# Forgetting attention's value matmuls with two heads in turn, and retention's scores in head order, in a two-layer hybrid decoder

## The chip, the core and the metric

One core of a Trainium2 chip runs the whole program: two decoder layers, one launch. The metric is the time of one execution in device microseconds (us). The core's engines work side by side, each through its own queue in order: PE (TensorE, with its weight loads, PEld), DVE (VectorE), ACT (ScalarE), POOL (GpSimd) and SP, which issues most DMAs. They wait for one another through semaphores.

## What is computed

The input is 512 tokens of width 1024; 16 learned meta tokens are put ahead of them. Each of two layers projects the normalized state, runs three mixers side by side (retention, a multi-scale pooling, and forgetting attention), projects their output, adds and normalizes, and then runs a SwiGLU. The reference for the parts that matter here, shortened:

```python
def retention_chunkwise(q, k, v):          # 4 heads, dk 48, dv 96, chunks of 128
    ...
    scores = jnp.einsum('bnihd,bnjhd->bnhij', qc, kc) * dmask
    inner = jnp.einsum('bnhij,bnjhe->bnihe', scores, vc)
    ...

def forgetting_attention(q, k, v, logf):   # 6 heads of 64, blocks of 128 queries
    ...
    def block(ib):
        s = jnp.einsum('bihd,bjhd->bhij', qb, kf)
        s = s + cb[..., :, None] - c[..., None, :]
        s = jnp.where(mask, s, NEG_INF)
        p = jax.nn.softmax(s, axis=-1)
        return jnp.einsum('bhij,bjhd->bihd', p, vf)
    ...
```

## The kernel before

The 528 positions are five chunks: chunk 0 holds the 16 meta tokens, chunks 1 to 4 hold 128 tokens each (`CH`). Two column halves, "A" (chunks 0 to 2) and "B" (3 and 4), go through the projections one after the other. Projection weights come in by DMA, are split by ACT (L188) and DVE or POOL (L140) into a high and a low part, and three matmuls (L241 to L243) do each product; these make up most of PE's work.

The order of PE's work is set by a planner. The program adds pieces with a cost in us, a priority, and for each dependency a lag (`LAG`); `Plan.run` keeps a clock of its own, takes at each step the ready piece of best priority, and adds its cost. It also counts what a piece holds until another has run (`holds`): buffers named "tmp" (7), "y" (23), "one" (PSUM banks) and so on. PE executes its instructions in this order (`manual_schedule`); the instructions of the other engines are issued by the same pieces. Projection pieces have priority 9 and attention pieces 5 and less, so projections fill the time in which attention has nothing ready.

Forgetting attention of chunk c (1 to 4) goes over six heads. For each head, `fox_score` makes the logits (two matmuls for each stretch of keys, L694 and L695), DVE adds the mask and finds the maximum (L739), ACT takes the exponential (L740), DVE normalizes (L741, L742) and POOL scales the meta tokens' share, pm (L743). `fox_turn` transposes the result in blocks of 128 keys (L751); DVE copies it back for even heads and ACT for odd ones (L753). `fox_value` multiplies it with the values of these c blocks (L761), one matmul for each block, adding up in PSUM. Each has 64 output rows: an even head writes partitions 0 to 63 and an odd one 64 to 127 of the same bank. Each fp32 matmul leaves two records in the trace. `fox_meta` adds the meta tokens' share (L774) and writes the result for the output projection (mixAf, mixBf). The copy of the transposed block of a head is held in a "tmp" buffer until its `fox_value` has run.

Retention of a chunk is `ret_score` (L816: four heads; heads 0 and 1 sit in rows 0 to 63 and 64 to 127 of one tile, heads 2 and 3 of another, and even heads write one PSUM bank, odd heads a second), `ret_out` and `ret_turn`; `ret_mix` later multiplies with the gate (L870) and splits the result for the output projection (ACT L872; the low part xl by DVE, or by POOL for the second of the three tiles). At the end of a mixing stage, `whole` adds the two parts of the layer's input on POOL (L420, 16 instructions), since the space is then reused for the mixers' output; `pool_mix` runs pooling's own matmuls (L901); and the output projection (L241 to L243 from mixAf, xh and xl) begins.

Of the kernel before, what the change touches and what calls it, by code (L numbers as in the profile page):

```python
# [17 lines left out]
P = 128  # L18
# [41 lines left out]
class Plan:  # L60
# [6 lines left out]
    def add(self, fn, cost=0.0, deps=(), prio=None):  # L67
        self.n += 1
        p = Piece(fn, cost, [d for d in (d if isinstance(d, tuple) else (d, 0.0) for d in deps) if d[0] is not None],
                  (5 if prio is None else prio, self.n))  # L70
        self.open.append(p)
        return p
# [34 lines left out]
def hymba_kernel(ctx: ExitStack, tc: tile.TileContext, d: dict, out: bass.AP):  # L107
    nc = tc.nc
# [21 lines left out]
    def one():  # L130
        return ps_one.tile([P, 512], F32, tag="one", name="one")
# [390 lines left out]
    def mixing(l, x, ready, ap_):  # L522

        def lag(k):
            return LAG.get(f"{k}_{l}", LAG[k])
# [10 lines left out]
        def tmp(name, shape=(P, NM + T), view=None):  # L536
            t = ap_.tile([P, NM + T], F32, tag="tmp", name=name, bufs=7)
            return t

        mix, F = {}, {}  # L540
# [13 lines left out]
        def open_mix():  # L554
            for half in "AB":
# [8 lines left out]
        vt = {"vf": ap_.tile([P, 4, 384], F32, tag="vtf", name="vtf"),  # L564
              "vr": ap_.tile([P, 5, 384], F32, tag="vtr", name="vtr")}
# [186 lines left out]
            pt = F[c, "pt", h] = ap_.tile([P, 512], F32, tag="tmp", name="pt", bufs=7)  # L752
            (nc.scalar.copy if h % 2 else nc.vector.tensor_copy)(pt[:, :nk], tp[:, :nk])  # L753

        def fox_value(c, h):
            nk = CH[c][1] - NM
            if h == 0:
                F[c, "o"] = one()
            o, pt = F[c, "o"], F.pop((c, "pt", h))
            for b in range(nk // P):  # L760
                nc.tensor.matmul(o[64 * (h % 2):64 * (h % 2) + 64, (h // 2) * P:(h // 2 + 1) * P],  # L761
                                 lhsT=vt["vf"][:, b, h * 64:(h + 1) * 64], rhs=pt[:, b * P:(b + 1) * P],
                                 start=(h < 2 and b == 0), stop=False, skip_group_check=True)

        def fox_meta(c, step):
            if step == 0:
# [42 lines left out]
        def ret_score(c):  # L809
            cs, ce = CH[c]  # L810
            n = ce - cs
            s = [one(), one()]
            for h in (0, 2, 1, 3):
                r0 = 64 * (h % 2)
                ab = "AB"[h // 2]
                nc.tensor.matmul(s[h % 2][:n, P * (h // 2):P * (h // 2) + n], lhsT=qk["k" + ab][r0:r0 + 64, cs:ce],  # L816
                                 rhs=qk["q" + ab][r0:r0 + 64, cs:ce], start=True, stop=True)
            if c:
                qx = R["qx", c] = tmp("qx")[:, :256].rearrange("p (j i) -> p j i", j=2)
                for j, ab in enumerate("AB"):  # L820
                    nc.vector.tensor_tensor(qx[:, j, :n], qk["q" + ab][:, cs:ce], C["xi"][:, j, :n], op=ALU.mult)
            pt = R["pt", c] = tmp("rpt")[:, :512].rearrange("p (b a i) -> p b a i", b=2, a=2)
            for b in range(2):
                nc.vector.tensor_tensor(pt[:n, b, :, :n], s[b][:n, :256].rearrange("p (a i) -> p a i", a=2)[:, :, :n],
                                        C["dm"][:n, b, :, :n], op=ALU.mult)
# [86 lines left out]
        def n_of(half, key):  # L912
# [3 lines left out]
        add = plan.add  # L916
# [10 lines left out]
        vf = {c: add(lambda c=c: v_turn("vf", c), 0.35, at(hf[c], "vt", *[("vf", i) for i in range(3)]), 3)  # L927
              for c in range(5)}
# [37 lines left out]
        if 0 in qch:  # L966
# [8 lines left out]
            b = add(lambda: fox_first(1), 0.05, [(a, lag("a"))], 5)  # L975
            mixes[0] = add(lambda: fox_first(2), 0.05, [(b, lag("b")), (vf[0], lag("v0")), oa], 5)
        prev_v, ss = None, [None, None]
        for c in range(1, 5):
            nk = ce = CH[c][1]
            for h in range(6):  # L980
                if h % 2 == 0:
                    qp = queries(c, h // 2)
                sc_ = add(lambda c=c, h=h: fox_score(c, h), 0.02 + max(ce, NA) / 1200.0,
                          at("AB"[:1 + (c > 2)], "kb", ("kf", h // 2))
                          + [(qp, lag("q")), ss[-1] if c == 4 else ss[-2]] + fb, 5)
                if h % 2:
                    qp.holds("Q", 1, sc_)
                ss.append((sc_, lag("s") + nk / 530.0))
                tn = add(lambda c=c, h=h: fox_turn(c, h), 0.11 * (nk // P), [(sc_, lag("p") + nk / 450.0)], 5)
                prev_v = add(lambda c=c, h=h: fox_value(c, h), 0.16 * (nk // P),  # L990
                             [(tn, lag("pt")), prev_v] + [(vf[b], lag("vt")) for b in range(1, c + 1)], 5)
                sc_.holds("tmp", 2, tn)
                tn.holds("tmp", 1, prev_v)
                if h == 0:
                    first_v = prev_v
            mt = add(lambda c=c: fox_meta(c, 0), 0.11, [(sc_, lag("p") + nk / 450.0)], 5)
            mixes[c] = prev_v = add(lambda c=c: fox_meta(c, 1), 0.65, [(mt, lag("mt")), prev_v, (vf[0], lag("v0"))]
                                    + [of if c > 2 else oa], 5)
            first_v.holds("one", 1, prev_v)
# [418 lines left out]
    with tc.tile_pool(name="at1", bufs=1) as ap_:  # L1418
        load_consts(1, ap_)
        x, ready, hs, keep = mixing(1, x, ready, ap_)  # L1420
# [122 lines left out]
```

## Time and profile before

| what | us |
|---|---|
| median of 3 runs | 1224.96 |
| lowest and highest run | 1223.85, 1227.76 |
| the profiled execution's own time | 1226.59 |
| its span, first to last instruction | 1224.8 |
| attention's value matmuls, L761, busy on PE | 30.3 |
| attention's transposes, L751, busy on PE | 21.3 |
| retention's scores, L816, busy on PE | 6.7 |

The span is one profiled execution; what lies around it is 1226.59 - 1224.8 = 1.8 us. A row of the timeline has the start in us from the span's start, the duration, the engine, the line and operation, out<-in by the program's names, and the count; where the engine sat idle before, the length and the releaser follow in brackets. Neighbouring matmuls overlap in the records, since a matmul's record lasts longer than the time after which the next can start. Where a row counts several, the duration is from the first start to the last end. A stretch's row has the busy time of each engine within it and, in brackets, its records.

### The profile page before, as it was taken

How to read it: one execution, taken by the hardware profiler on the slowest of the kernel's cores; microseconds unless marked ns; L12 is line 12 of the kernel's file. 1: busy time of each engine (PE TensorE's matmuls, PEld its weight loads, DVE VectorE, ACT ScalarE, POOL GpSimd, SP SyncE). 2: the span in 40 equal slices, each digit the busy share in tenths (PEclk: the TensorE clock that was granted, in tenths of full speed). 3: DMA queues.
4: the chain of work that ended last, by engine and by line, in shares of the span. 5: the costliest groups of instructions: out<-in, count | busy, mean ns of one | idle time of the engine just before them, and what ended most of it. 6: DMA issues, size and time to landing. Idle time of an engine off the chain costs nothing. (4 is left out here: it accounts for less than half of the span.)

```text
span 1224.8 us, 23583 instructions
## 1 busy us (share of the span) xinstructions
PE 1187.4 (97%) x9154; PEld 1135.8 (93%) x9154; DVE 833.3 (68%) x1762; ACT 600.7 (49%) x1178; POOL 322.1 (26%) x383
## 2 busy tenths in 40 slices
PE   7999999989999999999999899999999999999996
PEld 6999989989999999999999899999899999998885
DVE  6575686899885268864675655778897777763337
ACT  5535554466663236653355265445665555552222
POOL 5423446251110011100054243373311111100004
PEclk9999999999999999999999999999999999999999
DMA  6332201547762367732434221124477777532222
GB/s 240 108 107 70 71 18 58 170 135 177 193 162 81 100 186 180 179 82 84 130 114 130 80 74 59 43 91 160 139 193 198 181 181 181 140 115 91 93 96 69
DMA packets 58944, 151.90 MB, mean 124 GB/s; under 512 B 8328, under 2 KB 16808, under 8 KB 58832
## 3 DMA queue, kind: packets, MB, share of 16 engines
q1 hardware_dynamic: 47888, 130.46, 33.3%
q0 software_dynamic: 10944, 19.93, 10.1%
q8 instruction: 72, 1.18, 0.4%
q14 instruction: 40, 0.33, 0.1%
HBM read 144.38 MB, written 2.10 MB: 120 GB/s over the span
## 5 line engine op out<-in xcount | busy, mean ns | idle before, releaser
L241 PE MATMUL acc<-xh,w 128*128 128x256 f32 (+1 forms) x1024 | 299.7, 293 | 5.8 <-DVE ka L140 3.9
L242 PE MATMUL acc<-xl,w 128*128 128x256 f32 (+1 forms) x1024 | 291.3, 284 | 0.4 <-DVE xl L905 0.4
L243 PE MATMUL acc<-xh,w 128*128 128x256 f32 (+1 forms) x1024 | 291.3, 284 | 0.0
L140 DVE TENSOR_TENSOR w<-raw,w 128x1024 fp32r<-128x1024 f32 (+3 forms) x236 | 226.6, 978 | 68.2 <-ACT w L188 64.8
L188 ACT CAST w<-raw 128x1024 fp32r<-128x1024 f32 (+1 forms) x176 | 176.1, 1002 | 153.9 <-PE acc L243 86.5
L241 PEld LDWEIGHTS acc<-xh,w 128*128 128x128 f32 x1024 | 194.1, 190 | 10.7 <-issue 5.7
L242 PEld LDWEIGHTS acc<-xl,w 128*128 128x128 f32 x1024 | 194.1, 190 | 1.4 <-DVE xl L905 0.6
L243 PEld LDWEIGHTS acc<-xh,w 128*128 128x128 f32 x1024 | 193.9, 189 | 0.0
L1155 PE MATMUL acc<-xh,w 128*128 128x264 f32 (+1 forms) x608 | 121.9, 283 | 0.0
L202 POOL DMA_DIRECT2D raw<-in_w x38 | 33.4, 878 | 327.2 <-DMA raw<-in_w 88.0
L140 POOL TENSOR_TENSOR w<-raw,w 128x256 fp32r<-128x256 f32 (+1 forms) x60 | 88.3, 1478 | 94.1 <-ACT w L188 87.8
L1155 PEld LDWEIGHTS acc<-xh,w 128*128 128x128 f32 x608 | 98.5, 188 | 0.2 <-ACT g L1113 0.2
L1155 PE MATMUL acc<-xl,w 128*128 128x264 f32 (+1 forms) x304 | 85.6, 282 | 1.1 <-DVE xl L140 1.1
L140 DVE TENSOR_TENSOR S<-sr,S 128x512 fp32r<-128x512 f32 x76 | 52.3, 688 | 47.2 <-ACT S L211 46.4
L302 POOL TENSOR_TENSOR r<-r,mhalf 128x1 f32<-128x1 f32 (+3 forms) x18 | 14.8, 823 | 187.2 <-DVE r L301 187.2
L1155 PE MATMUL acc<-Th,S 128*128 128x264 f32 (+1 forms) x304 | 61.0, 283 | 1.0 <-ACT y L1105 1.0
L1155 PE MATMUL acc<-Th,w 128*128 128x264 f32 (+1 forms) x304 | 61.3, 284 | 0.0
L1155 PE MATMUL one<-Th,S 128*128 128x264 f32 (+1 forms) x304 | 61.1, 283 | 0.0
L1155 PE MATMUL one<-xh,S 128*128 128x264 f32 (+1 forms) x304 | 60.9, 283 | 0.0
L140 POOL TENSOR_TENSOR xl<-y,xh 128x256 fp32r<-128x256 f32 (+1 forms) x57 | 48.3, 857 | 45.8 <-ACT xh L317 39.8
L1155 PE MATMUL one<-xh,w 128*128 128x264 f32 (+1 forms) x304 | 60.2, 282 | 0.0
L1155 PEld LDWEIGHTS acc<-xl,w 128*128 128x128 f32 x304 | 57.2, 188 | 1.5 <-DVE xl L140 1.5
(558 smaller groups left out, 3087.3 us busy)
## 6 DMA issues: line engine op xcount, KB each, us to landing
raw<-in_w SPq DMA_DIRECT2D x88, 512.0 KB, 4.5
raw<-in_w_in SPq DMA_DIRECT2D x42, 512.0 KB, 3.8
raw<-in_w_out SPq DMA_DIRECT2D x32, 512.0 KB, 3.6
raw<-in_w2b SPq DMA_DIRECT2D x22, 512.0 KB, 3.3
s<-in_w SPq DMA_DIRECT2D x38, 256.0 KB, 3.6
s<-in_w POOLq DMA_DIRECT2D x38, 256.0 KB, 6.5
raw<-in_w POOLq DMA_DIRECT2D x38, 256.0 KB, 5.7
raw<-in_w2a SPq DMA_DIRECT2D x17, 512.0 KB, 3.9
```

Source lines behind the costliest of these rows:

```text
L140: return eng.tensor_tensor(lo, full, hi.bitcast(F32), op=ALU.subtract)
L188: nc.scalar.copy(w[:, 0, :n], raw[:, :n])
L202: nc.gpsimd.dma_start(a2[:, a], src1[:, a], accum_op=ALU.add)
L241: nc.tensor.matmul(ps, lhsT=wh, rhs=hi, start=first, stop=False)
L242: nc.tensor.matmul(ps, lhsT=wh, rhs=lo, start=False, stop=False)
L243: nc.tensor.matmul(ps, lhsT=wl, rhs=hi, start=False, stop=last)
L302: nc.gpsimd.tensor_tensor(r[:np_, :nb], r[:np_, :nb], mhalf[:np_, :nb], op=ALU.pow)
L1155: nc.tensor.matmul(ps, lhsT=a[:, w], rhs=b, start=fresh and k == 0 and q == 0, stop=k == 3 and q == 2, skip_group_check=True)
```

## The change

`fox_value` takes a pair of heads (2i and 2i+1) where it took one. It goes over the blocks of keys and, for each, issues the even head's matmul and then the odd head's. The planner's piece now depends on both heads' `fox_turn`, costs 0.26 us a block for the pair (0.16 for a head before), and both heads' copies are held until it has run. In `ret_score` the four heads are issued as 0, 1, 2, 3; before, as 0, 2, 1, 3. No instruction is added or removed.

```diff
-        def fox_value(c, h):
+        def fox_value(c, i):
+
             nk = CH[c][1] - NM
-            if h == 0:
+            if i == 0:
                 F[c, "o"] = one()
-            o, pt = F[c, "o"], F.pop((c, "pt", h))
+            o, pts = F[c, "o"], [F.pop((c, "pt", 2 * i + j)) for j in range(2)]
             for b in range(nk // P):
-                nc.tensor.matmul(o[64 * (h % 2):64 * (h % 2) + 64, (h // 2) * P:(h // 2 + 1) * P],
-                                 lhsT=vt["vf"][:, b, h * 64:(h + 1) * 64], rhs=pt[:, b * P:(b + 1) * P],
-                                 start=(h < 2 and b == 0), stop=False, skip_group_check=True)
+                for j, pt in enumerate(pts):
+                    h = 2 * i + j
+                    nc.tensor.matmul(o[64 * j:64 * j + 64, i * P:(i + 1) * P],
+                                     lhsT=vt["vf"][:, b, h * 64:(h + 1) * 64], rhs=pt[:, b * P:(b + 1) * P],
+                                     start=(i == 0 and b == 0), stop=False, skip_group_check=True)
...
             s = [one(), one()]
-            for h in (0, 2, 1, 3):
+            for h in range(4):
                 r0 = 64 * (h % 2)
...
-                prev_v = add(lambda c=c, h=h: fox_value(c, h), 0.16 * (nk // P),
-                             [(tn, lag("pt")), prev_v] + [(vf[b], lag("vt")) for b in range(1, c + 1)], 5)
                 sc_.holds("tmp", 2, tn)
+                if h % 2 == 0:
+                    even = tn
+                    continue
+                prev_v = add(lambda c=c, h=h: fox_value(c, h // 2), 0.26 * (nk // P),
+                             [(even, lag("pt")), (tn, lag("pt")), prev_v] + [(vf[b], lag("vt")) for b in range(1, c + 1)], 5)
+                even.holds("tmp", 1, prev_v)
                 tn.holds("tmp", 1, prev_v)
-                if h == 0:
+                if h == 1:
                     first_v = prev_v
```

The lines behind `fox_value` move by three, those of `ret_score` and behind it too, so L761 is L764 after, L816 is L819, L774 is L777 and L901 is L904.

On PE, at the first value matmuls of chunk 2 in layer 0 (pt_1981 is head 0's transposed block, pt_1986 head 1's), there stood:

```order
L723 MATMUL one_2009<-pt16_1699,vbd_140 128x16 x3
L774 MATMUL one_1903<-pmt_1817,vbd_140 128x128 x3
L761 MATMUL one_2020<-pt_1981,vtf_138 64x128 x2
L761 MATMUL one_2020<-pt_1986,vtf_138 64x128 x2
L751 MATMUL one_2025<-c_ident_94,p_1953 128x128 x2
L694 MATMUL one_2030<-ka_132,qa_1931 128x272
```

and now there stands:

```order
L723 MATMUL one_2009<-pt16_1699,vbd_140 128x16 x3
L777 MATMUL one_1903<-pmt_1817,vbd_140 128x128 x3
L764 MATMUL one_2020<-pt_1981,vtf_138 64x128
L764 MATMUL one_2020<-pt_1986,vtf_138 64x128
L764 MATMUL one_2020<-pt_1981,vtf_138 64x128
L764 MATMUL one_2020<-pt_1986,vtf_138 64x128
L751 MATMUL one_2025<-c_ident_94,p_1953 128x128 x2
L694 MATMUL one_2030<-ka_132,qa_1931 128x272
```

Head 1's first block has moved ahead of head 0's second. In most of chunks 2 to 4 the two heads' matmuls stood apart, with other pieces between; there the even head's have moved back to the odd head's.

On PE, at the start of layer 1's output projection (mixAf is its first input, pu the pooling's input), the end of the input projection was followed by:

```order
L241 MATMUL acc<-xh,w 128x256
L242 MATMUL acc<-xl,w 128x256
L243 MATMUL acc<-xh,w 128x256
L901 MATMUL one<-pu_7822,pw 128x256
L901 MATMUL one<-pu_7823,pw 128x256
L901 MATMUL one<-pu_7822,pw 128x256
L901 MATMUL one<-pu_7823,pw 128x256
L241 MATMUL acc<-mixAf,w 128x256
```

and now it is followed by:

```order
L241 MATMUL acc<-xh,w 128x256
L242 MATMUL acc<-xl,w 128x256
L243 MATMUL acc<-xh,w 128x256
L904 MATMUL one<-pu_7822,pw 128x256
L904 MATMUL one<-pu_7823,pw 128x256
L764 MATMUL one<-pt,vtf 64x128 x8
L904 MATMUL one<-pu_7822,pw 128x256
L904 MATMUL one<-pu_7823,pw 128x256
L777 MATMUL one<-pmt,vbd 128x128 x3
L241 MATMUL acc<-mixAf,w 128x256
```

Chunk 4's last value matmuls, of which head 5's stood 36 matmuls of the input projection ahead of its end, and the meta matmuls, which stood 24 ahead, have moved behind it. POOL's order at this place, with the rebuilt state (y, L420) behind the last four heads' pm, now reads

```order
L140 TENSOR_TENSOR w<-raw,w 128x1024
L743 TENSOR_SCALAR pm<-p,sm 128x16 x4
L420 TENSOR_TENSOR y<-xh,xl 128x256 x16
L140 TENSOR_TENSOR xl<-y,xh 128x256
L140 TENSOR_TENSOR w<-raw,w 128x1024
```

and differs from before only in the weight split in its first row, which stood two heads later.

## The prediction

> **What bounds the kernel now.** I read the page's first lines, then the busy time of every engine in the two stretches where forgetting attention runs (140 to 200 us in layer 0, 745 to 805 us in layer 1), with the fullest 35 us of each apart.
>
> ```profile
> span 1224.8 us, 23583 instructions
> PE 1187.4 (97%) x9154; PEld 1135.8 (93%) x9154; DVE 833.3 (68%) x1762; ACT 600.7 (49%) x1178; POOL 322.1 (26%) x383
> 140.00:200.00 60.00, 58.86 (x462) 52.55 (x461) 46.30 (x121) 30.32 (x76) 28.68 (x39) 1.00 0.15 45
> 745.00:805.00 60.00, 60.00 (x482) 54.68 (x480) 43.42 (x113) 31.09 (x76) 26.99 (x37) 1.00 0.13 43
> 145.00:180.00 35.00, 33.86 (x261) 29.65 (x260) 31.27 (x85) 19.43 (x52) 13.89 (x20) 1.00 0.10 31
> 755.00:790.00 35.00, 35.00 (x276) 31.20 (x274) 29.66 (x77) 18.65 (x49) 14.00 (x20) 1.00 0.10 31
> ```
>
> The columns after the stretch are PE, weight load, DVE, ACT and POOL busy, then the granted clock, which is full. PE has work nearly all the time: its queue is filled with projection matmuls wherever attention would wait. So a microsecond of PE work removed here is a microsecond of the run, as long as the other engines keep up. DVE is the one that may not: 31.27 of 35 us in the fullest part of layer 0, 29.66 of 35 in layer 1.
>
> **The value matmuls.** The same view for the value line alone, L761, one stretch for each chunk of queries 1, 2, 3, 4 of layer 0 and then of layer 1 (first number after the stretch: PE busy, with its matmul records; each fp32 matmul leaves two records, two passes):
>
> ```profile
> 140.00:142.00 2.00, 0.88 (x12) 0.63 (x12) 1.00 0.04 7
> 148.00:158.00 10.00, 2.63 (x24) 1.66 (x24) 1.00 0.17 56
> 160.00:175.00 15.00, 5.22 (x36) 3.77 (x36) 1.00 0.12 36
> 179.00:198.00 19.00, 6.53 (x48) 5.08 (x48) 1.00 0.12 32
> 747.00:749.00 2.00, 0.88 (x12) 0.63 (x12) 1.00 0.07 12
> 755.00:766.00 11.00, 3.04 (x24) 2.08 (x24) 1.00 0.11 34
> 766.00:779.00 13.00, 4.62 (x36) 3.41 (x36) 1.00 0.03 14
> 780.00:805.00 25.00, 6.53 (x48) 5.08 (x48) 1.00 0.14 43
> ```
>
> The 12 records of a chunk 1 take 0.88 us; in chunk 3 of layer 0, 36 records take 5.22. The timeline of PE shows why:
>
> ```profile
> 140.45 0.88 PE L761 MATMUL one<-pt,vtf 128*64 128x128 f32 x12
> ...
> 148.59 0.66 PE L761 MATMUL one<-pt,vtf 128*64 128x128 f32 x8
> ...
> 160.73 0.28 PE L242 MATMUL acc<-xl,w 128*128 128x256 f32 x1
> 160.84 0.28 PE L243 MATMUL acc<-xh,w 128*128 128x256 f32 x1
> 161.05 0.87 PE L761 MATMUL one<-pt,vtf 128*64 128x128 f32 x6
> 161.85 0.33 PE L751 MATMUL one<-c_ident,p 128*128 128x128 f32 x1
> ...
> 186.44 1.09 PE L761 MATMUL one<-pt,vtf 128*64 128x128 f32 x8
> ```
>
> At 161.05 one head's three blocks (6 passes) take 0.87 us; at 186.44 one head's four blocks (8 passes) take 1.09, so 0.11 a pass. But at 140.45 six heads with one block each, even and odd in turn, do 12 passes in 0.88, as long as six of one head. And at 148.59 two neighbouring heads of two blocks do 8 passes in 0.66. [...] What the change writes for a chunk 3 pair (six matmuls, even and odd in turn) is what already stands at 140.45.
>
> So the new cost of a pair: 0.66 in chunk 2, 0.88 in chunk 3, and in chunk 4 the 1.09 of one head plus 0.01 for the partner's later start, 1.10. Three pairs a chunk: 3 x (0.66 + 0.88 + 1.10) = 7.92 us a layer; chunk 1 stays (its three pairs still stand together). Layer 0 now pays 2.63 + 5.22 + 6.53 = 14.38, layer 1 pays 3.04 + 4.62 + 6.53 = 14.19. Saved: 6.46 + 6.27 = 12.73 us busy. A piece also costs something around its busy time: at 161.05 it starts 0.21 us after the matmul before it, where the row above has 0.11 (0.10 lost), and the next matmul starts 0.07 before the piece's modelled end, so 0.03 a piece. The order has 33 such pieces now and 20 after: 13 x 0.03 = 0.4. **PE loses 13.1 us of work.**
>
> **Retention's scores.** L816 in two of its nine pieces, layer 0's chunks 3 and 4:
>
> ```profile
> 93.00:95.00 2.00, 1.36 (x8) 1.03 (x8) 1.00 0.72 254
> 99.00:101.00 2.00, 0.72 (x8) 0.53 (x8) 1.00 0.00 0
> ```
>
> Eight passes, four on rows 0 to 63 and four on rows 64 to 127, take 0.72 us: they overlap already, though the order puts the two heads of each half one behind the other. Only the piece at 93 takes 1.36; its first matmul into the second PSUM bank has to wait for ACT, in both orders. I cost the new head order at nothing, with 1.36 - 0.72 = 0.64 as the most it can bring; were the cover gone, it would lose no more than that. [...]
>
> **What takes the place of the removed work.** Planner costs fall too (0.26 a block for a pair instead of 0.32), so PE pieces move closer to what they wait for. Three places.
>
> First, the softmax of each head runs PE, DVE, ACT, DVE, and then PE transposes. In layer 0 a transpose waits for it already; all 120 together wait 2.7 us:
>
> ```profile
> 171.02 0.55 PE L751 MATMUL one<-c_ident,p 128*128 128x128 f32 x3 [0.53 <-DVE p L742]
> ...
> L751 PE MATMUL one<-c_ident,p 128*128 128x128 f32 x120 | 21.3, 281 | 2.7 <-DVE p L742 2.2 <-DVE sm L741 0.5
> ```
>
> Between 145 and 180 us the change takes about 4 us from PE (0.7 in chunk 2, 2.6 in chunk 3, the rest in the first pair of chunk 4), which leaves 31 us for DVE's 31.27. At 100% DVE 0.3 us would be given back; if DVE stays at its 89%, all 4. I take 2.0, the middle: the waits would then about double. In layer 1 about 4.1 go from 755 to 790, 30.9 us are left for 29.66: bounds 0 and 4, and I take 0.5 as the share is still below 100%.
>
> Second, POOL at the end of the stage. It rebuilds x (L420, 16 instructions) right behind the last head's share of the meta tokens (pm, L743), and retention's low part of the output projection's input (xl) stands behind that in its queue, in both orders:
>
> ```profile
> 798.76 12.84 POOL L420 TENSOR_TENSOR y<-xh,xl 128x256 f32<-128x256 f32 x16
> 811.56 0.92 POOL L140 TENSOR_TENSOR xl<-y,xh 128x256 fp32r<-128x256 f32 x1
> ...
> 795.65 0.28 PE L695 MATMUL s<-kb,qb 66*128 66x256 f32 x1
> 795.77 0.28 PE L241 MATMUL acc<-xh,w 128*128 128x256 f32 x1
> ...
> 805.54 0.83 PE L774 MATMUL one<-pmt,vbd 96*128 96x128 f32 x6
> 806.13 0.36 PE L241 MATMUL acc<-xh,w 128*128 128x256 f32 x1
> ...
> 809.05 1.89 PE L901 MATMUL one<-pu,pw 128*128 128x256 f32 x8
> 810.58 0.47 PE L241 MATMUL acc<-mixAf,w 128*128 128x256 f32 x1
> ```
>
> In layer 1 the output projection starts 810.58 - 795.77 = 14.8 us after the last score. In the new order fewer pieces stand between: 42 projection matmuls at 0.117 (4.9), two transposes (0.8), pooling (1.5, 809.05 to 810.58), one value pair (1.1), the meta matmuls (0.6 from 805.54 to 806.13, 0.1 around them): 9.0 us. PE comes to the first matmul that reads xl of the second retention tile 36 matmuls later (4.4): 795.77 + 13.4 = 809.2 on the old clock. xl is there at 811.56 + 0.92 = 812.48. A wait of 3.3 us, from which goes the one that PE has there now:
>
> ```profile
> L242 PE MATMUL acc<-xl,w 128*128 128x256 f32 (+1 forms) x1024 | 291.3, 284 | 0.4 <-DVE xl L905 0.4
> ```
>
> That leaves 2.9; bounds 0 (DVE, less pressed, lets POOL go faster) and 3.3. Third, the same in layer 0:
>
> ```profile
> 190.86 12.98 POOL L420 TENSOR_TENSOR y<-xh,xl 128x272 f32<-128x272 f32 x16
> 204.60 0.78 POOL L140 TENSOR_TENSOR xl<-y,xh 128x272 fp32r<-128x272 f32 x1 [0.76 <-ACT xh L872]
> ...
> 188.44 0.28 PE L241 MATMUL acc<-xh,w 128*128 128x256 f32 x1
> ...
> 203.96 0.48 PE L241 MATMUL acc<-mixAf,w 128*128 128x272 f32 x1
> ```
>
> There more stays between: two value pairs instead of three single heads, and 48 projection matmuls instead of 72; about 11.7 us instead of 15.5 (3 us less of projection at 0.126, 0.9 less of values), so PE is at xl near 188.44 + 11.7 + 4.6 = 204.7, and xl can end at 190.86 + 12.98 + 0.78 = 204.6 if POOL need not wait for ACT, 205.4 as it is now. 0.3 of it.
>
> **The sum.** 13.1 - 2.0 - 0.5 - 2.9 - 0.3 = 7.4 us. Against the profiled execution, 1226.59 us, that is 1219.2. The median of the runs is 1224.96, 1.6 lower, and I predict on its scale: **1217.6 us**. All other stretches keep their order; they shift. About 0.3% (3.7 us) is what a measurement of this kernel can tell from no change.
>
> **The rivals.**
> - *Nothing is given back*: PE finds other work at the three places. Then 13.1, or 13.7 with the retention piece: 1211.3 to 1211.9. For it: 120 transposes wait only 2.7 us now. Against it: POOL's fixed 12.84 us. 0.14.
> - *DVE becomes the bound*: it keeps its 89% and 85%, so 4 + 4 are given back, with 3.2 at the ends: 13.1 - 11.2 = 1.9, 1223.1 us. For it: the wait at 171.02. Against: nothing says that DVE can't go over 89%. 0.11. [...]
> - *The pairs don't overlap*: then a pair costs one piece's start less, 2 x 0.87 - (0.87 + 6 x 0.11) + 0.03 = 0.24, by 13 pieces 3.1, less some 1 us for the overlaps that exist now: 1223. Against: 140.45 is the new order itself. 0.04. [...]
> - *Slower: the softmax's way sets the pace*. The value now waits for two heads, scores and transposes are ordered by costs that assume what the chains took before, and each of the 36 transposes of chunks 2 to 4 waits as the one at 171.02, 0.53 us: 19 us, 6 more than saved, 1231. It decides from 13.1 / 36 = 0.36 us a transpose. Against: all of them together wait 2.7 us now, and the planner still leaves the same lags between them. 0.07.
>
> **How the numbers follow.** My forecast has 0.64. Its own range, with the bounds of the three places, goes from 1212 to 1222. The range for 8 in 10 is 1211 to 1223.5, which takes in the first rival and most of the second. Faster by over 0.3% (below 1221.3): forecast and first rival, with a little of the second, 0.79. Slower 0.07. The rest, 0.14, within.
>
> **What would show it.** The value line's busy time should fall from 30.3 us (the sum of the eight stretches) to about 17.6; if it does not, the pairs don't overlap. A PE wait of about 3 us should stand at the start of layer 1's output projection, released by POOL's xl; if there is none, the second place is wrong. Waits of L751 for DVE's p in layer 0 should sum to about 2 us more than now, and DVE's share between 145 and 175 should be over 93%. The forecast is wrong if these waits exceed 9 us, or if a wait turns up outside the two attention stretches.

## Result and the profile after

The changed kernel takes 1232.78 us (median of 6 runs, 1230.45 to 1233.76) against 1226.15 us (1223.85 to 1228.09, 6 runs): ratio 1.0055, 95% interval 1.0044 to 1.0065. It is **slower by 0.55%**, 6.6 us. The forecast was 7.4 us faster.

The page's first lines (span, busy time of each engine, granted clock in 40 slices):

```profile
span 1231.7 us, 23577 instructions
PE 1180.1 (96%) x9154; PEld 1130.2 (92%) x9154; DVE 835.4 (68%) x1762; ACT 600.2 (49%) x1178; POOL 321.3 (26%) x383
PEclk9999998999999999999999999999999999999998
```

The stretches that the prediction showed (PE, weight load, DVE, ACT, POOL busy; granted clock), with 145 to 175 us added:

```profile
140.00:200.00 60.00, 52.19 (x417) 48.63 (x415) 43.79 (x117) 29.43 (x74) 22.55 (x28) 0.91 0.11 36
745.00:805.00 60.00, 55.35 (x463) 51.07 (x463) 43.05 (x107) 30.11 (x75) 22.99 (x29) 0.97 0.14 45
...
145.00:175.00 30.00, 26.27 (x210) 24.25 (x210) 22.25 (x65) 17.27 (x48) 13.59 (x20) 0.94 0.17 54
```

PE is busy 7.3 us less than before, and the run is longer: PE now waits, and its granted clock, 1.00 in both stretches before, is 0.91 and 0.97. DVE is not fuller; between 145 and 175 us its share is 74%. In before it was 89% there:

```profile
145.00:175.00 30.00, 28.86 (x219) 24.79 (x218) 26.79 (x72) 16.84 (x46) 12.33 (x17) 1.00 0.12 37
```

The values did what the change says. Busy time of the value line (L764) in the two attention stretches (140 to 220 and 740 to 830 us) together:

```profile
sum 170.00, PE 18.71 PEld 13.39; mean PE 9.35 PEld 6.70
```

One piece each of chunks 2, 3 and 4 from PE's timeline:

```profile
158.92 0.66 PE L764 MATMUL one<-pt,vtf 128*64 128x128 f32 x8
...
178.25 0.88 PE L764 MATMUL one<-pt,vtf 128*64 128x128 f32 x12
...
205.10 1.09 PE L764 MATMUL one<-pt,vtf 128*64 128x128 f32 x16
```

That is 18.71 us against 30.3, with the forecast prices of 0.66, 0.88 and 1.10 met. Where it went shows in PE's waits, between 140 and 220 us and between 740 and 830 us (total, times, longest):

```profile
PE one L751 <- DVE p L742: 7.6, 2, 4.1
PE acc L242 <- POOL xl L140: 0.5, 1, 0.5
...
PE one L751 <- DVE p L742: 3.4, 1, 3.4
PE one L904 <- DVE xl L908: 1.1, 1, 1.1
...
PE acc L242 <- POOL xl L140: 0.4, 1, 0.4
```

Three waits of the transposes for a softmax result make 11.0 us: at 166, 188 and 785 us. DVE's and POOL's timelines at the first of them, and PE's:

```profile
158.56 0.57 DVE L739 CUSTOM_DVE_ANT_0 p<-one,mask 128x400 f32<-128x400 f32 x1
...
159.05 0.93 DVE L883 TENSOR_TENSOR pb<-pu 128x543 f32<-128x543 f32 x1
...
162.14 0.69 DVE L896 SCALAR_TENSOR_TENSOR pu<-pc,pu 64x512 f32<-64x512 f32 x1
162.86 0.17 DVE L895 TENSOR_TENSOR pu<-pt,pu 64x16 f32<-64x16 f32 x1
162.95 0.56 DVE L739 CUSTOM_DVE_ANT_0 p<-one,mask 128x400 f32<-128x400 f32 x1
...
163.44 2.50 DVE L742 TENSOR_SCALAR p<-p,sm 128x384 f32<-128x384 f32 x1
...
163.39 2.34 POOL L140 TENSOR_TENSOR w<-raw,w 128x1024 fp32r<-128x1024 f32 x1 [0.49 <-ACT w L188]
...
162.06 0.49 PE L751 MATMUL one<-c_ident,p 128*128 128x128 f32 x3
166.09 0.64 PE L751 MATMUL one<-c_ident,p 128*128 128x128 f32 x3 [3.54 <-DVE p L742]
```

The head whose mask step (L739) starts at 158.56 has its last softmax step (L742) only at 163.44, because the pooling branch's running sums (L883 to L896), and then the next head's mask step, stand ahead in DVE's queue; and that step, 0.41 to 0.42 us in ten of the eleven others of its width, then takes 2.50, as long as POOL's weight split beside it (the low part of a chunk of the output projection's weights, 2.34). At the wait at 785 us it is one of the sums ahead of the step that is stretched, 0.68 us elsewhere (DVE, then POOL):

```profile
779.68 2.85 DVE L896 SCALAR_TENSOR_TENSOR pu<-pb,pu 64x512 f32<-64x512 f32 x1
...
779.40 2.58 POOL L140 TENSOR_TENSOR w<-raw,w 128x1024 fp32r<-128x1024 f32 x1 [0.40 <-ACT w L188]
```

Each wait is followed by a slow clock, as the stretches behind the three show (columns as above):

```profile
165.90:170.00 4.10, 3.91 (x19) 3.78 (x20) 3.30 (x11) 1.91 (x5) 1.59 (x3) 0.58 0.40 128
188.30:193.00 4.70, 4.51 (x20) 4.34 (x20) 1.73 (x6) 1.31 (x4) 0.57 (x1) 0.50 0.01 3
784.40:789.00 4.60, 4.45 (x30) 4.15 (x31) 4.54 (x12) 1.59 (x4) 0.79 (x1) 0.65 0.09 33
```

At 0.58, 0.50 and 0.65 of full speed these stretches lose an estimated 4.10 x 0.42 + 4.70 x 0.50 + 4.60 x 0.35 = 5.7 us. So the 30.3 - 18.7 = 11.6 us that the value matmuls save stand against 11.0 + 5.7 given back and some 2 us of small new waits: about 7 us slower by this estimate. Measured from the first value matmul to the first matmul of the output projection (140.45 to 203.96 and 747.22 to 810.58 us before, 142.69 to 209.90 and 751.43 to 817.18 now), layer 0 takes 3.7 us longer and layer 1 2.4, together 6.1.

Two other differences of the two profiles nearly cancel, and the runs don't tie them to the change. The changed one has lost 2.2 us ahead of its first value matmul, with a wait of 1.2 us at 72 us; e7 below, with the same order up to there, starts its first value matmul at 140.34. And before has a slow stretch of its own behind 684 us (4.5 us at 0.62), which the changed one lacks; e7 has it (0.64) and e1, on before, has not.

### The profile page after: what moved, and what is told of

Read it like the earlier page. It is cut to its first block, busy times and chain, and to the rows that moved or that the text cites. A ratio compares the mean times of both kernels' runs of the same rounds, so it can differ in the third digit from the quotient of the medians.

```text
span 1231.7 us, 23577 instructions
## 1 busy us (share of the span) xinstructions
PE 1180.1 (96%) x9154; PEld 1130.2 (92%) x9154; DVE 835.4 (68%) x1762; ACT 600.2 (49%) x1178; POOL 321.3 (26%) x383
## 5 line engine op out<-in xcount | busy, mean ns | idle before, releaser
L242 PE MATMUL acc<-xl,w 128*128 128x256 f32 (+1 forms) x1024 | 292.6, 286 | 0.9 <-POOL xl L140 0.9
L140 DVE TENSOR_TENSOR w<-raw,w 128x1024 fp32r<-128x1024 f32 (+3 forms) x236 | 230.3, 994 | 68.8 <-ACT w L188 65.5
L241 PEld LDWEIGHTS acc<-xh,w 128*128 128x128 f32 x1024 | 195.6, 191 | 11.6 <-issue 6.6
L242 PEld LDWEIGHTS acc<-xl,w 128*128 128x128 f32 x1024 | 195.6, 191 | 2.2 <-POOL xl L140 1.7
```

Of the source, the lines that this page charges most:

```text
L140: return eng.tensor_tensor(lo, full, hi.bitcast(F32), op=ALU.subtract)
L241: nc.tensor.matmul(ps, lhsT=wh, rhs=hi, start=first, stop=False)
L242: nc.tensor.matmul(ps, lhsT=wh, rhs=lo, start=False, stop=False)
```

## The experiments

Eighteen kernels, each timed beside the kernel before on the same chip. The runs in one view (ratio to before):

| run | us | ratio | interval |
|---|---|---|---|
| the change | 1232.78 | 1.0055 | 1.0044 to 1.0065 |
| e1_order_only | 1226.53 | 1.0002 | 0.9992 to 1.0013 |
| e3_wout_split_dve | 1228.94 | 1.0030 | 1.0019 to 1.0041 |
| e4, the same on before | 1227.14 | 1.0011 | 1.0001 to 1.0021 |
| e5_sums_late | 1233.29 | 1.0069 | 1.0054 to 1.0084 |
| e7_pairs_serial | 1235.88 | 1.0096 | 1.0073 to 1.0119 |
| e11_pt_on_act | 1233.49 | 1.0069 | 1.0054 to 1.0084 |
| e12_sums1_late | 1236.68 | 1.0087 | 1.0065 to 1.0109 |
| e13, the same on before | 1230.66 | 1.0040 | 1.0025 to 1.0055 |
| e14_sums_place_of_before | 1230.64 | 1.0036 | 1.0023 to 1.0050 |
| e15_before_sums_moved | 1226.36 | 1.0005 | 0.9994 to 1.0015 |
| e16_place_and_split | 1225.28 | 0.9995 | 0.9982 to 1.0009 |
| e17_more_room | 1239.87 | 1.0115 | 1.0098 to 1.0133 |
| e18_more_room_split | 1234.08 | 1.0066 | 1.0045 to 1.0086 |
| e19_sums_bounds_split | 1225.13 | 0.9998 | 0.9983 to 1.0013 |
| e20_place_room_split | 1223.85 | 0.9982 | 0.9972 to 0.9991 |
| e21_place_quarters | 1224.21 | 0.9986 | 0.9977 to 0.9995 |
| e22_place_room_quarters | 1228.22 | 1.0015 | 1.0006 to 1.0025 |
| e23_place_room3_split | 1221.87 | 0.9964 | 0.9950 to 0.9977 |

### The two parts of the change

The score order alone, on before:

```diff
-            for h in (0, 2, 1, 3):
+            for h in range(4):
```

> The kernel before with the retention heads in the order 0, 1, 2, 3 and nothing else changed. Theory A (the loss comes from the softmax chain in forgetting attention): the head order is free, ratio to before 0.999 to 1.001, PE starts shifted by less than 0.4 us at 130 us. Rival (the 2.2 us by which the changed kernel was late at 94 to 140 us, ahead of any value matmul that was touched, come from the head order): about 2 us slower, 1.0015 to 1.003, with a PE wait near 72 us for the DVE write of ka (0.3 us in before, 1.47 in after).

1.0002: it is free. The wait near 72 us isn't there in this run; it comes and goes, and isn't a matter of the order.

The pairs without the alternation, on the changed kernel:

```diff
-            for b in range(nk // P):
-                for j, pt in enumerate(pts):
-                    h = 2 * i + j
+            for j, pt in enumerate(pts):
+                h = 2 * i + j
+                for b in range(nk // P):
```

> The changed kernel with the matmuls of a pair head by head (all blocks of the even head, then those of the odd one); every other engine's order is as in the changed kernel. By 0.11 us a pass the value pieces then cost 0.88, 1.32 and 1.76 us in chunks 2, 3 and 4 instead of 0.59, 0.81 and 1.02, about 9 us more PE work in all. Theory A' (between 155 and 190 us and around 785 us DVE's queue sets the pace and PE's shorter values only wait longer): the three waits shrink by most of what lies ahead of them, and the time stays within 3 us of the changed kernel, 1231 to 1236 us. Rival F (the alternation brings its full 9 us, and the loss comes from something else, the pairing or the planner's order): 1240 to 1243 us with the three waits as long as before.

A piece of chunk 3 and one of chunk 4 on PE's timeline:

```profile
174.88 1.15 PE L764 MATMUL one<-pt,vtf 128*64 128x128 f32 x12
...
202.19 1.58 PE L764 MATMUL one<-pt,vtf 128*64 128x128 f32 x16
```

The value line's busy time in the two stretches together:

```profile
sum 170.00, PE 23.63 PEld 18.64; mean PE 11.81 PEld 9.32
```

The waits for p in layer 0 and in layer 1:

```profile
PE one L751 <- DVE p L742: 7.6, 2, 4.1
...
PE one L751 <- DVE p L742: 3.3, 1, 3.3
```

My price for a serial pair was wrong: 16 passes take 1.58 us, not 1.76; 8 of one head take 1.09, so the two heads' passes overlap here too. Pairing alone brings 30.3 - 23.6 = 6.7 us of PE work and alternating another 4.9. The time differs by 1.0096 - 1.0055, 5.0 us, with intervals that leave 2 to 8: PE's shorter values do become time, and the three waits don't depend on how long a value piece is. Theory A' falls by its waits, though 1235.88 us lies in its range; rival F is right about the waits, and its 1240 to 1243 us came from the wrong price.

### POOL's split, the sums, and DVE's load

The splits of chunks 0 and 1 of the output projection's weights go from POOL to DVE by two entries of CFG:

```diff
-o0=1, o1=1, o2=0,
+o0=0, o1=0, o2=0,
```

> The changed kernel with the low parts of output-projection chunks 0 and 1 computed on DVE instead of POOL; PE's order is the same. Theory A (a 2.4 us POOL weight split stretches the DVE instruction that runs beside it, and PE runs dry behind the softmax chain): the three PE waits of 3.8, 4.4 and 3.7 us at 166, 188 and 785 us fall below 1 us each, the granted clock stays at 1.00 there, and the time falls by 10 to 16 us, to 1217 to 1223 us, below the kernel before. Rival B (DVE simply has too much work, or the pair has to wait for its second head): DVE gets four splits of about 1.2 us more to do in these stretches, so the waits stay or grow and the time is 1232 us or more.

> The same edit on the kernel before. Theory A: there PE hardly waited in these stretches (0.53 us at 171), so the edit brings at most 2 us: 1224 to 1228 us, ratio 0.998 to 1.002. Rival (the edit helps any kernel by itself, by what comes later in POOL's queue): it gains as much here as on the changed kernel.

The waits of the changed kernel with this, in layer 0 and layer 1:

```profile
PE one L751 <- DVE sm L741: 3.5, 1, 3.5
PE one L751 <- DVE p L742: 1.8, 2, 1.4
...
PE one L751 <- DVE p L742: 2.4, 1, 2.4
```

7.7 us instead of 11.0, and 0.25% gained, where before loses 0.1% by the same edit. That is neither theory A's 10 to 16 us nor rival B's longer waits. The first wait falls by the 2.1 us of the stretch, as theory A has it; the second keeps 3.5 (DVE now has each split in its own queue; one of this shape takes it 1.24 us on average in before). So the split is one cause of at least two. On the changed kernel, then, both halves of the sums (`[ss[-1]]`) or the second alone (`* m`) behind the last score; the second alone on before, too:

```diff
-        us_ = {m: add(lambda m=m: pool_sums(m), 0.0, both(("u", m)), 5) for m in range(2)}
+        us_ = {m: add(lambda m=m: pool_sums(m), 0.0, both(("u", m)) + [ss[-1]] * m, 5) for m in range(2)}
```

> The changed kernel with the running sums of the pooling branch (DVE) put behind the last attention score, instead of amid the chunks 3 and 4; the POOL splits stay where they are. Theory A: what the split stretches is then mostly not the sums that stand ahead of a softmax step, the waits at 166, 188 and 785 us shrink from 11.9 us together to below 5, and the time falls by 6 to 12 us, 1221 to 1227 us. Rival C (the split alone does it, whatever stands beside it): one of the three waits at most shrinks, 1229 to 1233 us. Rival D: the sums are the cause by their own length and come late for the pooling matmuls: a new PE wait of 2 us or more at L904 ahead of the output projection.

> The changed kernel with only the second half of the pooling sums (m = 1) behind the last attention score; the first half stays at 159 us. Theory A'/G: the waits at 188 and 785 us go (8.1 us and the lowered clock behind them, some 2 us), the one at 166 us stays, and as the first half is done early the pooling matmuls wait far less than with both halves late (there 14.4 us), at most 3 us a layer: 1222 to 1228 us. Rival H (the second half late is as costly at the end as it was amid the chunk): new waits at L904 of 4 us or more in each layer, 1230 us or more.

> The same edit on the kernel before, where nothing waited for the sums. Theory A': it brings nothing, 1224 to 1229 us, ratio 0.998 to 1.003; any wait at L904 is a loss. Rival: it gains as much here as on the changed kernel (4 us or more), so that the place of the sums costs in both.

Both halves late, PE's waits in layer 0, then in layer 1:

```profile
PE one L904 <- DVE pu L895: 8.3, 2, 5.6
PE one L751 <- DVE sm L741: 1.0, 1, 1.0
PE one L751 <- DVE p L742: 0.4, 1, 0.4
...
PE one L904 <- DVE pu L896: 4.9, 1, 4.9
```

The waits for the softmax fall from 11.0 to 1.4 us, though the splits stay: L742 at 161.52 takes 2.51 us beside one, and without the sums in the queue PE hardly notices. But the sums are then late for the pooling matmuls (L904), 13.2 us: rival D. With the second half alone late, the wait at 188 us goes, that at 785 stays at 3.4, and new ones come at L904 (2.7, in layer 0 alone) and at layer 1's output projection (2.1 and 3.6): rival H's time, with other waits than it named. The same edit costs before 0.4%, more than I expected.

Less work for DVE, by the even heads' copies of pt on ACT:

```diff
-            (nc.scalar.copy if h % 2 else nc.vector.tensor_copy)(pt[:, :nk], tp[:, :nk])
+            nc.scalar.copy(pt[:, :nk], tp[:, :nk])
```

> The changed kernel with the even heads' copies of the transposed weights (pt) on ACT instead of DVE, so that DVE loses about 13 copies of 0.4 to 0.7 us in each layer. PE's order is the same. Theory A': DVE has about 5 us less to do between 145 and 205 us, the three waits fall from 11.9 us to 6 or less together, and the time falls to 1222 to 1228 us. Rival G (not DVE's total work counts, but the block of pooling sums and the stretched instruction right ahead of a softmax step): the waits stay within 2 us of 11.9 and so does the time, 1230 to 1234 us; ACT's longer queue can make it worse.

Nothing gained: 7.0 us of such waits in layer 0 (3.5 and 3.5), 4.0 in layer 1. That is rival G's forecast: here DVE's total doesn't count, but what stands in one block ahead of the step that PE needs.

### Is it the place of the sums?

In before the sums stand behind chunk 2's and chunk 3's last score in layer 0; in the changed kernel behind chunk 3's second and chunk 4's first. The edit puts them where a table says, and holds the next chunk's first score until they are issued:

```diff
+        us_, at_, hold = {}, {(0, 2, 5): 0, (0, 3, 5): 1, (1, 4, 1): 1}, {(0, 3, 0): 0, (0, 4, 0): 1}
+        def sums(m, *deps):
+            if m not in us_:
+                us_[m] = add(lambda: pool_sums(m), 0.0, both(("u", m)) + list(deps), 5)
...
-                          + [(qp, lag("q")), ss[-1] if c == 4 else ss[-2]] + fb, 5)
+                          + [(qp, lag("q")), ss[-1] if c == 4 else ss[-2], us_.get(hold.get((l, c, h)))] + fb, 5)
+                if (l, c, h) in at_:
+                    sums(at_[l, c, h], sc_)
...
-        us_ = {m: add(lambda m=m: pool_sums(m), 0.0, both(("u", m)), 5) for m in range(2)}
         for m in range(2):
+            sums(m)
```

> The changed kernel with the pooling sums put back to where they stood among the softmax steps of before: in layer 0 the first half behind chunk 2's last score (and chunk 3's first score held until then), the second half behind chunk 3's last; in layer 1 the second half behind chunk 4's second score, the first half where it is (behind chunk 3's last score in both kernels). Theory P (the loss is the place of the sums, about 5 us of DVE in one block, ahead of the softmax step that PE needs next): layer 0's waits at 166 and 188 us (8.2 us) shrink to 2 us or less together and the clock stays at 1.00 there; in layer 1 the wait at 785 us stays between 1 and 3.7 us. Time 1220 to 1226 us, faster than before or level. Rival Q (PE, with 10 us less in the values, reaches the softmax too early wherever the sums stand): the waits move but still sum to 8 us or more, 1230 us or more.

The mirror image has the table {(0, 3, 1): 0, (0, 4, 0): 1} and no hold, on before.

> The mirror image: the kernel before, its single-head values untouched, with layer 0's sums put where the changed kernel has them (first half behind chunk 3's second score, second half behind chunk 4's first). Theory P: two PE waits for the DVE write of p appear in layer 0, 4 to 8 us together, and the time rises to 1230 to 1236 us though nothing of the change is in it. Rival Q: with the old, slower values PE is late enough that nothing waits, 1224 to 1228 us.

By its numbers rival Q comes out in both: put back, the sums leave waits for p of 4.0 us in layer 0 (four, longest 2.1) and 5.1 in layer 1, 9.1 together, at 1230.64 us; moved in before, they cost nothing (1226.36). Their place isn't without effect either: layer 0's waits nearly halve, and the ratio is 1.0036 instead of 1.0055, though the two intervals overlap a little. So their place alone doesn't slow a kernel; the changed order is more exposed to it. One thing e15 leaves open: its POOL splits start at 165.53 and 180.53 us, when the heads behind the sums have their p, where the changed kernel has them at 163.39 and 182.00, ahead of it. Before as it is has both ahead of one head, chunk 3's head 5 (the split at 165.32, the sums from 167.85), and PE waits 0.5 us for it. The starts of the records show what the heads had. For the head behind the sums, us from its last score matmul until p is written (need) and until its transposes start, less their wait (room):

| kernel, head | score | need | room |
|---|---|---|---|
| changed, layer 0, chunk 3 head 1 | 157.93 | 8.0 | 4.6 |
| changed, layer 0, chunk 4 head 1 | 179.54 | 8.8 | 4.9 |
| changed, layer 1, chunk 3 head 5 | 775.94 | 8.5 | 5.2 |
| before, layer 0, chunk 3 head 5 | 164.81 | 6.2 | 5.7 |
| before, layer 0, chunk 4 head 0 | 169.44 | 7.2 | 7.3 |
| before, layer 1, chunk 3 head 5 | 769.66 | 4.8 | 5.5 |
| before with moved sums, chunk 3 head 1 | 155.12 | 5.5 | 6.9 |
| before with moved sums, chunk 4 head 1 | 174.40 | 6.2 | 5.7 |

The changed order leaves 4.6 to 5.2 us where that of before leaves 5.5 to 7.3, and the need has grown, about 2 us of it by the stretch. In layer 0 both have their part. In layer 1 the first half of the sums stands behind chunk 3's head 5 in both kernels, and the room hardly differs (5.2 and 5.5); there the need makes the wait. POOL's split starts amid these sums, at 779.40, and in before at 778.29, 3 us behind the last of them.

### Two causes at once, and more room

The placed sums with the splits on DVE, as above:

> The changed kernel with the sums placed as in before and, too, the low parts of output-projection chunks 0 and 1 on DVE instead of POOL. Theory P with the stretch by POOL as a second cause: layer 1's wait near 785 us shrinks as well (it is behind a 2.85 us DVE instruction that takes 0.68 alone), 2 to 4 us less than the placed kernel without this, 1217 to 1223 us. If the stretch doesn't matter once the sums stand well: within 1 us of the placed kernel or slower by DVE's own splits of 1.2 us.

The whole loss is healed (0.9995), with 1.4 us of waits for p left in layer 0 and 3.9 in layer 1 (in its fastest execution, 1222.81 us, which is the one profiled); no gain yet, 2 us short of theory P's range. Of all the runs this one shows best that the two causes together make the loss. Then more planned time for the heads that waited, with the sums where the change has them, and the splits on POOL or DVE:

```diff
-                tn = add(lambda c=c, h=h: fox_turn(c, h), 0.11 * (nk // P), [(sc_, lag("p") + nk / 450.0)], 5)
+                tn = add(lambda c=c, h=h: fox_turn(c, h), 0.11 * (nk // P), [(sc_, lag("p") + nk / 450.0 + {(0, 3, 1): 4.0, (0, 4, 1): 4.5, (1, 3, 5): 4.0, (1, 4, 0): 4.5}.get((l, c, h), 0.0))], 5)
```

> The changed kernel with a longer planned time from score to transposes for the four heads whose softmax is served behind the pooling sums (layer 0: chunk 3 head 1 by 4.0 us, chunk 4 head 1 by 4.5; layer 1: chunk 3 head 5 by 4.0, chunk 4 head 0 by 4.5). The first half of layer 0's sums and both halves in layer 1 keep their place in DVE's order; DVE, ACT and POOL do the same work. Theory R (the loss is a plan that leaves 4.5 to 5.2 us between score and transposes where the softmax behind sums and split takes 7.7 to 8.5): PE does projection work meanwhile, the three waits of 11.9 us fall to 3 or less together, the clock stays at 1.00, and the time falls to 1218 to 1226 us. Rival S (DVE cannot keep up in these stretches whatever PE's order is): the waits come back at later heads, 1229 us or more.

> As the kernel with more room for four heads, and the low parts of output-projection chunks 0 and 1 on DVE instead of POOL. Theory R with the stretch as a second cause: with the room there already the stretch hardly reaches PE, so this gains little on the other, 0 to 3 us, 1216 to 1224 us. If the stretch is what remains: 3 us or more better.

The first is the slowest of all, 1239.87 us. Its waits in layer 0:

```profile
PE one L751 <- DVE p L742: 8.2, 3, 4.0
PE one L904 <- DVE xl L908: 3.2, 1, 3.2
```

Theory R falls in this form: the planner let the next head's transposes pass the delayed ones, and these waited for a softmax just as late (rival S). In layer 1 the waits for p go, and one of 2.4 us for POOL's pm comes. The edit also moved layer 0's second half of the sums, so it is no clean test of the room alone. With the splits on DVE 5.8 us of it are gone: here the stretch weighs more than I expected. The next two keep the splits on DVE. One has the sums at the chunk bounds in both layers (tables {(0, 2, 5): 0, (0, 3, 5): 1, (1, 2, 5): 0, (1, 3, 5): 1} and {(0, 3, 0): 0, (0, 4, 0): 1, (1, 3, 0): 0, (1, 4, 0): 1}); the other has them as in before and 2.5 us more for (1, 3, 5) and (1, 4, 0).

> The changed kernel with the sums behind the last score of chunk 2 and of chunk 3 in both layers (in layer 1 too, where they stood behind chunk 3's last score), the next chunk's first score held until then, and the splits of chunks 0 and 1 on DVE. Theory R: in layer 1 the wait near 772 us of 2.65 us in the kernel placed in layer 0 alone goes or falls below 1.5 us; time 1219 to 1224 us. If layer 1 has the wait wherever the sums stand: 1225 us as before.

> The changed kernel with the sums placed as in before, the splits of chunks 0 and 1 on DVE, and 2.5 us more planned time for layer 1's chunk 3 head 5 and chunk 4 head 0 alone. Theory R: against the same without the added time (1225.3 us) the waits in layer 1 of 2.65 and 1.8 us shrink to 1.5 together, 1220 to 1224 us. Rival S: nothing gained, 1225 us or more.

0.9998: layer 1 waits about as much with the sums at the bounds (2.2 us at 767, 1.9 at 785 from start to start; this profile is of the slowest of its ten executions, 1231.23 us, so its waits may be more than usual). 0.9982: the added time brings 1.4 us, which the intervals don't tell from nothing, and one wait of 3.1 us is left at 789 us. Last, the splits on POOL in four instructions of 256 columns each, without and with that added time, and the added time for (1, 4, 2) too, with the splits on DVE (of the splits' line, the part that changes):

```diff
-nc.gpsimd if CFG[f"o{m}"]
+(quarters if m < 2 else nc.gpsimd) if CFG[f"o{m}"]
```

> The changed kernel with the sums placed as in before and the low parts of output-projection chunks 0 and 1 still on POOL, each in four instructions of 256 columns instead of one of 1024. Theory T (a DVE instruction with both sources in SBUF can't end before the POOL instruction that runs beside it, so what counts is the length of POOL's instruction): DVE's softmax and sums instructions beside the pieces take 1.2 us at most instead of 1.9 to 2.85, the waits in layer 0 and at 779 us shrink, and the time lies near the kernel with the splits on DVE (1225.3), 1224 to 1227 us. Rival U (POOL holds DVE off for the whole run of pieces): 1230 us, as with one long instruction (1230.6), or slower by the pieces' extra fixed cost.

> As the kernel before in this list, with 2.5 us more planned time for layer 1's chunk 3 head 5 and chunk 4 head 0. Theory T: about 1.5 us better than without the added time, 1221 to 1225 us, level with or below the best so far (1223.9). Rival U: 1228 us or more.

> The best so far (sums placed as in before, splits of chunks 0 and 1 on DVE, 2.5 us more for two heads of layer 1; 1223.9 us, with a wait of 3.1 us left at 789 us for chunk 4's head 2) and 2.5 us more for that head. If that wait is filled with projection work: 1219 to 1222.5 us, faster than before by more than 0.3%. If it comes back at the next head, as with more room in layer 0: 1223 to 1226 us.

The timelines of DVE and POOL at the first split, with one instruction (e14):

```profile
162.26 2.55 DVE L742 TENSOR_SCALAR p<-p,sm 128x384 f32<-128x384 f32 x1
...
162.22 2.37 POOL L140 TENSOR_TENSOR w<-raw,w 128x1024 fp32r<-128x1024 f32 x1
```

The same with four (e21):

```profile
162.22 0.92 DVE L742 TENSOR_SCALAR p<-p,sm 128x384 f32<-128x384 f32 x1
163.06 0.56 DVE L739 CUSTOM_DVE_ANT_0 p<-one,mask 128x400 f32<-128x400 f32 x1
...
162.19 2.92 POOL L140 TENSOR_TENSOR w<-raw,w 128x256 fp32r<-128x256 f32 x4
```

Its waits for p in layer 0:

```profile
PE one L751 <- DVE p L742: 1.7, 3, 0.9
```

Theory T's forecast holds: the same step takes 0.92 instead of 2.55 us, the waits for p in layer 0 fall from 4.0 to 1.7, and the kernel gains 6.4 us, though POOL's split itself takes longer. The added time on top is a miss (1228.22): at 773 us PE waits 2.6 us for POOL's pm, where it waited 2.5 for ACT's p without the added time, and at 790 a wait of 3.0 us for p is new. With the splits on DVE and (1, 4, 2) added, the time pays: **1221.87 us, 0.9964 (0.9950 to 0.9977), faster than both kernels**, with these waits left in layer 1:

```profile
PE one L751 <- DVE p L742: 1.5, 2, 0.8
PE one L904 <- DVE xl L908: 1.3, 1, 1.3
```

In its profile layer 0 takes 5.1 us less than in before from the first value matmul to the output projection, and layer 1 1.0 less: 6.1 of the 11.6 us. In layer 1, PE still waits 4.3 us there in all, where before waits 0.4.

## Why the prediction was wrong

- *What bounds the kernel.* PE, right. That DVE may not keep up was right in name only: I read it as a rate (31.27 of 35 us), and its share fell to 74% where I forecast over 93%.
- *The value matmuls.* Right in the overlap and in size: 18.71 us for 17.6. Most of the difference lies in three pieces, at 193, 773 and 796 us: the first took 1.39 us at a granted clock of 0.77, the other two, which waited 0.17 and 0.40 us for ACT's pt amid the pair, 1.27 and 1.52. The rival in which pairs don't overlap fell: the piece at 158.92 does its 8 passes in 0.66 us, where 8 of one head took 1.09, and the weight loads are busy for 0.42 of the same 0.66.
- *Retention's scores.* Right: nothing.
- *The step that failed* is "what takes the place of the removed work", first place. I took 2.0 us for layer 0 and 0.5 for layer 1, from the middle of shares over 35 us; it was 7.6 and 3.4, in three waits. What counted was the block ahead of one step in DVE's queue, against the time that PE's order leaves that head (a need of 8.0 to 8.8 us against a room of 4.6 to 5.2). In layer 0 the sums moved in that queue relative to the scores, and in layer 1 POOL's split moved onto them (the orders of DVE and POOL can be read before any run); I never asked where they came to stand. E16, with the sums put back and the splits on DVE, takes the whole loss away.
- *The stretch by POOL* was missing. Its row stood in the trace of before:

```profile
165.80 2.13 DVE L742 TENSOR_SCALAR p<-p,sm 128x384 f32<-128x384 f32 x1
...
165.32 2.39 POOL L140 TENSOR_TENSOR w<-raw,w 128x1024 fp32r<-128x1024 f32 x1 [0.45 <-ACT w L188]
```

  Behind this step came three of the sums, and then the wait at 171.02 that I quoted and charged to DVE's load. E3 against the change and e21 against e14 show what the stretch is worth: 3 to 6 us.
- *The clock* was missing: an estimated 5.7 us behind the three waits.
- *Second and third place.* The second was mis-sized: of 2.9 us by POOL's xl at layer 1's output projection 0.4 came, at L242, and 1.1 by DVE's xl at L904. That POOL goes faster beside a less pressed DVE, the reason of the bound of 0, no run shows apart; POOL's rebuild took 12.22 us instead of 12.84. The 0.3 in layer 0 were 0.5. Why the second wait was so short was not tried: PE had waited before, but it is 0.4 in e23 too, where it had waited far less.
- *The rival on the other side* had the place (transposes waiting for the softmax) and the sign; its mechanism, 36 small waits of 0.53 us, was not it. The text's own sign of a wrong forecast, over 9 us of these waits, was set too high: it named layer 0, which had 7.6, and only both layers together pass it, with 11.0.
- *A sum.* The forecast's own range, to 1222, doesn't follow from the bounds of the places: 4 + 4 + 3.3 and 0.3 give back 11.6 of 13.1, which ends at 1223.5. The measured time lies far outside either.

What stays open: how need and room share the blame in layer 0 of the changed order. E17 meant to add room alone and changed the order as well. Why the order brings two heads' scores within 0.4 us of each other (157.56 and 157.93 in chunk 3; 156.12 and 157.99 for neighbours before) was not tried; that the pair's two pt buffers come free together is a guess.

## What to carry to other kernels

Where the bound engine loses work, follow each step that it will reach earlier back through the queue of its producer, instruction by instruction, and compare the longest block there with the time that the new order leaves; DVE's busy share said nothing about it here (74% now, with the waits, and 89% before). Look for instructions that are far longer than others of their form, and at what runs beside them: cutting one long instruction into four was worth 6 us here (e21 against e14), and moving DVE's copies to ACT nothing (e11). A wait on TensorE like the three here (3.4 to 4.1 us) is to be priced with the stretch behind it, which ran at a granted clock of 0.50 to 0.65.

## What the runs showed of the hardware

**Two DVE instructions ended with POOL's.** In the changed kernel L742 (one source and its result in SBUF) and L894 (two sources in SBUF) end with POOL's 1024-column subtraction (165.94 and 165.73 us; 184.67 and 184.64); L624, one of whose two sources is in PSUM, took 0.41 us beside it, and 0.41 to 0.44 in all its instances:

```profile
182.31 0.41 DVE L624 SCALAR_TENSOR_TENSOR y<-y,acc 128x256 f32<-128x256 f32 x1
182.74 1.93 DVE L894 TENSOR_TENSOR pt<-pc,c_icnt 64x16 f32<-64x16 f32 x1
...
182.00 2.64 POOL L140 TENSOR_TENSOR w<-raw,w 128x1024 fp32r<-128x1024 f32 x1 [0.99 <-ACT w L188]
```

L894 takes 0.17 us in its other three instances. POOL starts first in these rows (182.00 and 182.74; 163.39 and 163.44); L896, which started ahead of it at 181.70, took its usual 0.68 us. Why the two are stretched and L624 is not, and with it theory T's condition of two sources in SBUF, no run tried apart. What the length of POOL's instruction did was tried: beside one of 1024 columns L742 took 2.55 us (e14), beside four of 256 columns 0.92 (e21).

**The clock behind gaps in PE's work.** In the 20 profiles of this study, between 140 and 830 us, the granted clock of the 4.5 us behind a gap from one PE start to the next was below 0.9 (at 0.50 to 0.69) for none of 88 gaps from 1.2 to 1.8 us, for 2 of 26 from 1.8 to 2.2, for 20 of 34 from 2.2 to 3.2, and for 20 of 21 above 3.2 us (not for one of 3.81 us, in e7). A gap of 2.55 us was followed by 0.62 in before (683.87), and one of 2.53 us by 1.00 in the changed kernel (689.76): what decides between 2.2 and 3.2 us, the runs don't show.

**Matmuls of two heads overlap without being alternated**: 16 passes of a serial pair take 1.58 us (e7), two single heads 2 x 1.09 (before, 186.44).
